# ScalarE divides the wide softmax tiles, and the engines' order is planned anew

## The chip, the core and the metric

The kernel runs on one core of a Trainium2 chip. A core has five engines that run their own queues of instructions in order and meet at semaphores: TensorE (PE in the profile; PEld is its weight load), VectorE (DVE), ScalarE (ACT), GpSimd (POOL) and SyncE (SP), which issues the DMAs. The metric is the time of one execution on the device, in microseconds.

## What is computed

One decoder layer on 512 rows of width 1024 in float32: a norm, one input projection into 17 parts, four groups of four attention heads of width 64, gates, and an output projection. Cut to what matters:

```python
hn = rms_norm(x, norm_gain)
proj = jnp.einsum('btd,de->bte', hn, w_in)
(fq, fk, fv, ff, fg, mq, mk, mv, mg, sq, sk, sv, sg, wq, wk, wv, wg) = split_columns(proj)
# f, m, w heads: s = q.k * scale + bias (forget sums, distance table, distance table in a window)
p = jax.nn.softmax(s, axis=-1).astype(v.dtype)
o = jnp.einsum('bhqk,bhkd->bhqd', p, v)
# s heads: a = exp(log_sigmoid(z) + suffix sums of log_sigmoid(-z)) below the diagonal
y = jnp.concatenate([from_heads(o_fox) * jax.nn.silu(fg), from_heads(o_moba) * jax.nn.silu(mg),
                     from_heads(o_sb) * jax.nn.silu(sg), from_heads(o_swa) * jax.nn.silu(wg)], axis=-1)
return x + jnp.einsum('bte,ed->btd', y, w_out)
```

In the softmax heads the division by the row sum is the step that the change is about.

## The kernel before

Each float32 operand of a large product is split into a high half (written by ScalarE in `hi_copy`, L137) and a low half (the difference, written by `lo_part` on VectorE, L142 or L144, or by GpSimd, L252). A product is then three matmuls (`mm3`, L340 to L342). The weights come in 39 chunks; for the chunks in `POOL_LO` GpSimd makes the low half in pieces of up to 260 columns, for all others VectorE does in one instruction. Names follow this: `wh_mqk0` and `wl_mqk0` are the halves of chunk 0 of the m heads' query and key weights, `raw_mqk0` what was loaded.

The work goes projection by projection (`ORDER`), and the heads of group s, then f, m and w run between the projections' matmuls. A head works through four query blocks. For block i of an f or m head the tile is 512, 384, 256 and 128 columns wide, for a w head at most 256. In `softmax_head` VectorE adds the bias and takes the row maximum (L548), ScalarE takes the exponential and its row sum (L550), VectorE takes the reciprocal of the sum (L555) and multiplies the tile by it (L556). The tile `pm` is then transposed on TensorE (`pT`, L522), split (`pth` by ScalarE, `ptl` by VectorE) and multiplied with V (`o`, L472 and L473). An s head has a chain of its own: scores on TensorE (`s_s`, L509 with the high half of k, L510 with the low half), three activations, a prefix sum by VectorE (`pm_s`, L592), a subtraction (L593) and an exponential (L594).

`pair_out` multiplies two heads' output by their gate on GpSimd (`oc`, L491) and splits it into `yh` (ScalarE) and `yl` (VectorE). The output projection starts with the six pairs of s, f and m (`out_tile`, tiles `o100`, `o101`, and so on) while the w heads run, and ends with the two pairs of w.

What the code writes down is not the order in which the engines run it. `order_engines` takes all instructions, and `_plan` lays them out anew, engine by engine, as a list schedule: each step has a cost from `_Step.cost`, a delay `_LAT` from engine to engine, an extra `MARGIN` for some receivers, and a priority, which is its place in the code plus an offset from `TURN`. A step may be taken before an earlier ready one if it can start within `PATIENCE` of it. VectorE and GpSimd read the on-chip memory through a port that they share; steps marked `port` take turns at it in the plan. The order found is then fixed by dependences, so that a table of numbers sets it.

Of the kernel before, what the change touches and what calls it, by code (L numbers as in the profile page):

```python
# [12 lines left out]
AF = mybir.ActivationFunctionType  # L13
ALU = mybir.AluOpType
# [24 lines left out]
REL_AT = "fg"  # L39
SQK_BANKS, R_BANK = ["sc", "tp", "tp", "pv"], "pj"  # L40

RATE, OUTU = 4.54, 0.55

POOL_LO = {1, 4, 6, 9, 10, 12, 15, 16, 17, 19, 21, 23, 24, 34, 36, 37, 38}
PIECE = 260
DVE_SQ = {(1, 1), (2, 1), (3, 0), (3, 1)}

OCUT, WARM, WARM_GAPS = 2, 3, 8


TURN = {"xn": 207, "gate": 18, "qk": -250, "v": -71, "s": 14, "pt": -313, "ot": 134, "gap":
        100000, "y": 10, "fb": 5, "w": 108, "pv": 16, "oc": 186, "nat": 0, "proj": 61, "x": -110}
PATIENCE = {"Pool": 10, "PE": 54}

MARGIN = {"PE": 100, "Activation": 41}


BOUNDS = list(range(17)) + [21, 27, 35, 46, 59, 77, 99, 128, 166, 216, 280, 363, 470]
# [18 lines left out]
def block_kernel(ctx, tc, x, xT, w_in, w_out, small, rel, out):  # L77
    nc = tc.nc
# [72 lines left out]
    if WARM:  # L151
# [3 lines left out]
        pt = pv("warm")  # L155
# [64 lines left out]
    def advance():  # L220
# [23 lines left out]
        for a0 in range(0, ka, ka // cut):  # L244
# [17 lines left out]
    xn = [[sb.tile([P, 512], F32, tag="yh", name=f"x{t}{h}", bufs=9) for h in range(2)]  # L262
          for t in range(NT)]
# [267 lines left out]
    def softmax_head(g, h, Q, K, V, vcol, bias, nblk):  # L531
        pm = sb.tile([P, 1280], F32, tag="pm", name=f"pm_{g}{h}", bufs=2)
        off, blocks = 0, {}
        for i in range(NT):
            w = nblk(i)
            n = w * P
            blocks[i] = (off, w)
            s, s2 = scores(g, h, i, n, Q, K)
            seg = pm[:, off:off + n]
            b = bias(i, n)  # L540
            if s2 is not None:
                nc.vector.tensor_tensor(seg, s2, b, op=ALU.add)
                b = seg
            nm = cp.tile([P, 1], F32, tag="nm", name=f"nm_{g}{h}{i}", bufs=4)
            sm = cp.tile([P, 1], F32, tag="sm", name=f"sm_{g}{h}{i}", bufs=4)

            init = nsk[:, h:h + 1] if g == "w" else 3.0e38
            nc.vector.tensor_tensor_reduce(seg, s, b, scale=-1.0, scalar=init,  # L548
                                           op0=ALU.add, op1=ALU.min, accum_out=nm)
            nc.scalar.activation(seg, seg, AF.Exp, scale=-1.0, bias=nm, accum_out=sm)  # L550
            if g == "w":
                es = cp.tile([P, 1], F32, tag="es", name=f"es_{g}{h}{i}", bufs=2)
                nc.scalar.activation(es, sk[:, h:h + 1], AF.Exp, bias=nm)
                nc.vector.tensor_tensor(sm, sm, es, op=ALU.add)
            nc.vector.reciprocal(sm, sm)  # L555
            nc.vector.tensor_scalar(seg, seg, sm, None, op0=ALU.mult)  # L556
            off += n
            yield
        for res in pt_tiles(g, h, pm, blocks):
            yield  # L560
        out_half(g, h, finish_head(g, h, res, V, vcol))
        yield
# [348 lines left out]
class _Step:  # L911
# [20 lines left out]
    def cost(self):  # L932
        n = self.writes[0].cols if self.writes else 1
        if self.eng == "PE":
            if "const" in self.reads[0].name:
                return n * 8 / 2.4
            if "float32r" in str(self.ins.ins[0].dtype):
                return n * 0.422 + 11
            return 112 if any("ident" in a.name for a in self.reads) else n * 4 / 2.4 + 11
        if self.kind == "DMACopy":  # L940
            return 1040 if self.eng == "Pool" else 60
# [94 lines left out]
def _plan(steps, moved, held_back, turn, patience, margin):  # L1036
# [23 lines left out]
    prio = [s.k + sum(turn.get(n, 0) for n in moved.get(s.ins.name, ())) for s in steps]  # L1060

    def start(e, k):
        t = max(free[e], ready[k])
        return max(t, port[other[e]]) if steps[k].port else t

    plan = []
    for _ in steps:
        t, e = min((start(e, k), e) for e in can for k in can[e])
        _, k, t = min((prio[k], k, start(e, k)) for k in can[e]
                      if start(e, k) <= t + patience.get(e, 0))  # L1070
        s = steps[k]
        can[s.eng].remove(k)
        src, end = s.eng, t + s.cost()
        plan.append((s, t, end))
# [68 lines left out]
```

## Time and profile before

| | us |
|---|---|
| median of 3 runs (lowest, highest) | 290.74 (290.61, 292.94) |
| the profiled execution | 290.52 |
| its span, first to last instruction | 288.7 |
| TensorE busy | 280.4 |
| VectorE busy | 233.6 |
| ScalarE busy | 193.8 |
| GpSimd busy | 89.5 |

The span is what the engines' instructions cover; the 1.8 us beside it lie before the first and after the last instruction. A matmul's row in the profile lasts longer than the time to the next one (0.39 us for 512 columns, where the next starts 0.23 us later), since matmuls are pipelined; short waits therefore do not show as idle time of PE, but as idle time of PEld, whose next load stands still.

### The profile page before, as it was taken

The page shows a single profiled execution, that of the slowest core. Times are in us where ns is not written, and L with a number is a line of the kernel's source. Part 1 is how long each engine was busy: PE and PEld are TensorE (multiplying, and loading weights), DVE is VectorE, ACT ScalarE, POOL GpSimd, SP SyncE. Part 2 cuts the span into 40 slices and gives each one's busy share as a digit, 9 for nine tenths or more (in the row PEclk, how much of TensorE's full clock was granted, in tenths as well). Part 3 has the DMA queues.
Part 4 walks back from the last instruction along what each step waited for, and adds up shares of the span by engine and source line. Part 5 has one row for each costly group of instructions (what it writes and reads, how often), then busy time and mean ns, then how long its engine had stood idle before and what let it go on. Part 6 is the DMA issues. An engine that isn't in the chain of part 4 may idle for free.

```text
span 288.7 us, 4641 instructions
## 1 busy us (share of the span) xinstructions
PE 280.4 (97%) x1529; PEld 235.9 (82%) x1529; DVE 233.6 (81%) x606; ACT 193.8 (67%) x445; POOL 89.5 (31%) x140
## 2 busy tenths in 40 slices
PE   8999998999999899999999999999999999999995
PEld 8998888888887678887798988788888886888884
DVE  2869289888998897669999789776989979996653
ACT  4784288957895947288895669569957877765300
POOL 5608045320029562135494000006200656001010
PEclk9999999999999999999999999999999999999999
DMA  7996342251023259621155240514001545200024
GB/s 236 333 400 191 116 151 76 70 176 44 0 74 105 95 152 287 171 73 38 41 143 148 73 145 2 183 36 145 3 18 72 173 138 168 89 2 0 2 110 182
DMA packets 19960, 33.65 MB, mean 117 GB/s; under 512 B 1616, under 2 KB 10068, under 8 KB 19808
## 3 DMA queue, kind: packets, MB, share of 16 engines
q1 hardware_dynamic: 19504, 32.96, 36.9%
q10 hardware_dynamic: 432, 0.39, 0.5%
q8 instruction: 12, 0.20, 0.3%
q14 instruction: 12, 0.10, 0.1%
HBM read 31.22 MB, written 4.22 MB: 123 GB/s over the span
## 4 chain that ended last, share of the span: by engine, by line
PE 68%; DVE 20%; ACT 8%; DMA 2%; issue 1%; ACTq 0%
PE o L342 5%; PE o L341 5%; PE o L340 4%; DVE pm_s L592 3%; PE p_wqkv L342 3%; PE p_wqkv L341 3%; PE p_wqkv L340 3%; PE p_sqk L341 2%; PE p_sqk L340 2%; PE p_sqk L342 2%; PE p_fqk L341 2%; PE p_fqk L340 2%; PE p_fqk L342 2%; DMA raw_sv<-in_w_in 2%; PE pT_m L522 2%; DVE pm_f L548 1%
## 5 line engine op out<-in xcount | busy, mean ns | idle before, releaser
L252 POOL TENSOR_TENSOR wl_fqk<-raw_fqk,wh_fqk 128x260 fp32r<-128x260 f32 (+1 forms) x12 | 11.8, 1010 | 18.9 <-ACT wh_fqk L137 18.9
L491 POOL TENSOR_TENSOR oc_f<-oc_f,gate_f 128x512 f32<-128x512 f32 x2 | 2.6, 1297 | 43.1 <-ACT gate_f L754 43.1
L676 POOL TENSOR_SCALAR fxb<-fbc,scol 128x512 f32<-128x512 f32 (+3 forms) x16 | 10.4, 654 | 17.4 <-DVE qs_f L144 10.4
L592 DVE TENSOR_TENSOR_SCAN pm_s<-l 128x512 f32<-128x512 f32 (+3 forms) x16 | 15.0, 942 | 0.1
L252 POOL TENSOR_TENSOR wl_sg<-raw_sg,wh_sg 128x256 fp32r<-128x256 f32 x8 | 7.0, 914 | 25.0 <-ACT wh_sg L137 25.0
L342 PE MATMUL p_fqk<-wh_fqk,xl 128*128 128x512 f32 x32 | 12.8, 401 | 0.0
L340 PE MATMUL p_mqk<-wh_mqk,xh 128*128 128x512 f32 x32 | 12.8, 400 | 0.0
L340 PE MATMUL p_wqkv<-wh_wqkv,xh 128*128 128x512 f32 x32 | 12.8, 399 | 0.0
L341 PE MATMUL p_mqk<-wl_mqk,xh 128*128 128x512 f32 x32 | 12.8, 399 | 0.0
L340 PE MATMUL p_fqk<-wh_fqk,xh 128*128 128x512 f32 x32 | 12.7, 403 | 0.0
L341 PE MATMUL p_fqk<-wl_fqk,xh 128*128 128x512 f32 x32 | 12.7, 397 | 0.0
L341 PE MATMUL p_wqkv<-wl_wqkv,xh 128*128 128x512 f32 x32 | 12.7, 396 | 0.0
L342 PE MATMUL p_mqk<-wh_mqk,xl 128*128 128x512 f32 x32 | 12.7, 396 | 0.0
L342 PE MATMUL p_wqkv<-wh_wqkv,xl 128*128 128x512 f32 x32 | 12.7, 396 | 0.0
L340 PE MATMUL p_sqk<-xh,wh_sqk 128*128 128x512 f32 x32 | 12.5, 389 | 0.0
L341 PE MATMUL p_sqk<-xl,wh_sqk 128*128 128x512 f32 x32 | 12.3, 390 | 0.0
L342 PE MATMUL p_sqk<-xh,wl_sqk 128*128 128x512 f32 x32 | 12.2, 392 | 0.0
L491 POOL TENSOR_TENSOR oc_w<-oc_w,gate_w 128x512 f32<-128x512 f32 x2 | 2.6, 1290 | 29.9 <-DVE oc_w L486 29.9
L142 DVE TENSOR_TENSOR ptl_s<-pT_s,pth_s 128x384 fp32r<-128x384 f32 (+3 forms) x16 | 7.4, 484 | 4.9 <-ACT pth_s L137 4.8
L142 DVE TENSOR_TENSOR ptl_m<-pT_m,pth_m 128x384 fp32r<-128x384 f32 (+3 forms) x16 | 7.3, 484 | 4.1 <-ACT pth_m L137 4.1
L137 ACT ACTIVATE pth_m<-pT_m 128x384 fp32r<-128x384 f32 (+3 forms) x16 | 6.5, 435 | 5.6 <-PE pT_m L522 5.4
L594 ACT ACTIVATE pm_s<-pm_s 128x512 f32<-128x512 f32 (+3 forms) x16 | 7.3, 465 | 4.1 <-DVE pm_s L593 3.9
(354 smaller groups left out, 1118.9 us busy)
## 6 DMA issues: line engine op xcount, KB each, us to landing
raw_o<-in_w_out SPq DMA_DIRECT2D x8, 512.0 KB, 3.2
xT<-in_xT SPq DMA_DIRECT2D x8, 256.0 KB, 4.1
raw_sqk<-in_w_in SPq DMA_DIRECT2D x4, 512.0 KB, 5.9
x<-in_x SPq DMA_DIRECT2D x8, 256.0 KB, 6.0
raw_fqk<-in_w_in SPq DMA_DIRECT2D x4, 512.0 KB, 3.7
raw_mqk<-in_w_in SPq DMA_DIRECT2D x4, 512.0 KB, 3.6
raw_wqkv<-in_w_in SPq DMA_DIRECT2D x4, 512.0 KB, 3.6
xr<-in_x SPq DMA_DIRECT2D x4, 512.0 KB, 3.8
```

What stands on the lines that cost most here:

```text
L137: nc.scalar.activation(dst, src, AF.Copy if isinstance(scale, float) else AF.Identity, scale=scale)
L142: nc.vector.tensor_tensor(dst, src, hi.bitcast(F32), op=ALU.subtract)
L252: nc.gpsimd.tensor_tensor(lv[q], rv[q], hv[q].bitcast(F32), op=ALU.subtract)
L340: nc.tensor.matmul(dst, ah, bh, start=first, stop=False)
L341: nc.tensor.matmul(dst, ah, bl, start=False, stop=False)
L342: nc.tensor.matmul(dst, al, bh, start=False, stop=last)
L491: nc.gpsimd.tensor_tensor(oc, oc, gates[e], op=ALU.mult)
L522: nc.tensor.transpose(pt[:, a * P:(a + 1) * P], pm[:, o:o + P], ident)
L548: nc.vector.tensor_tensor_reduce(seg, s, b, scale=-1.0, scalar=init, op0=ALU.add, op1=ALU.min, accum_out=nm)
L592: nc.vector.tensor_tensor_scan(seg, l, l, 0.0, ALU.add, ALU.bypass)
L594: nc.scalar.activation(seg, seg, AF.Exp)
L676: nc.gpsimd.tensor_scalar(b, bc[:, i * P:], -1.0, scol[:, i, h:h + 1], op0=ALU.mult, op1=ALU.add)
```

## The change

The diff does three things. In `softmax_head` tiles wider than 256 columns are multiplied by the reciprocal on ScalarE, with the reciprocal as the scale of an activation; these are the blocks of 512 and 384 columns of the eight f and m heads, 16 instructions. Of the chunks whose low half GpSimd makes, 6 (`fvf0`) and 17 (`mqk0`) go to VectorE and 32 (`o1`) comes from it (there is no chunk 39). And the planner gets other numbers: `TURN`, `PATIENCE`, `MARGIN` and `OUTU` change, a matmul of few columns costs more, and a step that takes the shared port waits `LEAD` longer before it on GpSimd. The instructions are otherwise the same; only their order changes. Lines of the changed file are numbered 2 higher before the new branch and 5 higher behind it.

```diff
--- before.py
+++ after.py
@@ -39,20 +39,22 @@
 REL_AT = "fg"
 SQK_BANKS, R_BANK = ["sc", "tp", "tp", "pv"], "pj"
 
-RATE, OUTU = 4.54, 0.55
-
-POOL_LO = {1, 4, 6, 9, 10, 12, 15, 16, 17, 19, 21, 23, 24, 34, 36, 37, 38}
+RATE, OUTU = 4.54, 0.4
+
+POOL_LO = {1, 4, 9, 10, 12, 15, 16, 19, 21, 23, 24, 32, 34, 36, 37, 38, 39}
 PIECE = 260
 DVE_SQ = {(1, 1), (2, 1), (3, 0), (3, 1)}
 
 OCUT, WARM, WARM_GAPS = 2, 3, 8
 
 
-TURN = {"xn": 207, "gate": 18, "qk": -250, "v": -71, "s": 14, "pt": -313, "ot": 134, "gap":
-        100000, "y": 10, "fb": 5, "w": 108, "pv": 16, "oc": 186, "nat": 0, "proj": 61, "x": -110}
-PATIENCE = {"Pool": 10, "PE": 54}
-
-MARGIN = {"PE": 100, "Activation": 41}
+TURN = {"xn": 207, "gate": 101, "qk": -250, "v": -54, "s": 14, "pt": -313, "ot": 322, "gap":
+        100000, "y": 7, "fb": 5, "w": 81, "pv": -31, "oc": 258, "nat": 0, "proj": 59, "x": -110}
+PATIENCE = {"Pool": 10, "PE": 54, "Activation": 29}
+
+MARGIN = {"PE": 100, "Activation": 52}
+
+LEAD = {"Pool": 120, "DVE": 0}
 
 
 BOUNDS = list(range(17)) + [21, 27, 35, 46, 59, 77, 99, 128, 166, 216, 280, 363, 470]
@@ -553,7 +555,10 @@
                 nc.scalar.activation(es, sk[:, h:h + 1], AF.Exp, bias=nm)
                 nc.vector.tensor_tensor(sm, sm, es, op=ALU.add)
             nc.vector.reciprocal(sm, sm)
-            nc.vector.tensor_scalar(seg, seg, sm, None, op0=ALU.mult)
+            if n > 256:
+                nc.scalar.activation(seg, seg, AF.Copy, scale=sm)
+            else:
+                nc.vector.tensor_scalar(seg, seg, sm, None, op0=ALU.mult)
             off += n
             yield
         for res in pt_tiles(g, h, pm, blocks):
@@ -935,7 +940,7 @@
             if "const" in self.reads[0].name:
                 return n * 8 / 2.4
             if "float32r" in str(self.ins.ins[0].dtype):
-                return n * 0.422 + 11
+                return max(n * 0.4167 + 15, 109)
             return 112 if any("ident" in a.name for a in self.reads) else n * 4 / 2.4 + 11
         if self.kind == "DMACopy":
             return 1040 if self.eng == "Pool" else 60
@@ -1060,15 +1065,20 @@
     prio = [s.k + sum(turn.get(n, 0) for n in moved.get(s.ins.name, ())) for s in steps]
 
     def start(e, k):
+
         t = max(free[e], ready[k])
-        return max(t, port[other[e]]) if steps[k].port else t
+        if not steps[k].port:
+            return t, t
+        t += LEAD[e]
+        return max(t, port[other[e]]), t
 
     plan = []
     for _ in steps:
-        t, e = min((start(e, k), e) for e in can for k in can[e])
-        _, k, t = min((prio[k], k, start(e, k)) for k in can[e]
-                      if start(e, k) <= t + patience.get(e, 0))
+        (t, _), e = min((start(e, k), e) for e in can for k in can[e])
+        _, k, t = min((prio[k], k, start(e, k)[0]) for k in can[e]
+                      if start(e, k)[0] <= t + patience.get(e, 0))
         s = steps[k]
+        t -= LEAD[e] if s.port else 0
         can[s.eng].remove(k)
         src, end = s.eng, t + s.cost()
         plan.append((s, t, end))
```

On VectorE, at the first scores of the s heads, before the change (qs_s and k are the low halves of queries and keys, sqk3 the last of the four projected tiles that they are made from):

```order
L144 SCALAR_TENSOR_TENSOR qs_s01_450<-sqk0_445,qs_s01_450 64x512
L144 SCALAR_TENSOR_TENSOR qs_s10_480<-sqk1_478,qs_s10_480 64x512
L144 SCALAR_TENSOR_TENSOR qs_s11_483<-sqk1_478,qs_s11_483 64x512
L142 TENSOR_TENSOR k00_138<-sqk2_511,k00_138 64x512
L142 TENSOR_TENSOR k01_140<-sqk2_511,k01_140 64x512
L786 TENSOR_TENSOR sqk3_574<-p_sqk3_519,rrow_135 128x512
L739 TENSOR_SCALAR fsp_151<-p_fvf0_582,rx_129 128x4
L586 TENSOR_TENSOR s_s00_612<-s_s00_612,smask_146 128x128
```

and after it:

```order
L146 SCALAR_TENSOR_TENSOR qs_s01_448<-sqk0_443,qs_s01_448 64x512
L791 TENSOR_TENSOR sqk3_572<-p_sqk3_517,rrow_135 128x512
L744 TENSOR_SCALAR fsp_151<-p_fvf0_580,rx_129 128x4
L146 SCALAR_TENSOR_TENSOR qs_s10_478<-sqk1_476,qs_s10_478 64x512
L146 SCALAR_TENSOR_TENSOR qs_s11_481<-sqk1_476,qs_s11_481 64x512
L144 TENSOR_TENSOR k00_138<-sqk2_509,k00_138 64x512
L144 TENSOR_TENSOR k01_140<-sqk2_509,k01_140 64x512
L144 TENSOR_TENSOR k10_142<-sqk3_572,k10_142 64x512
L144 TENSOR_TENSOR k11_144<-sqk3_572,k11_144 64x512
L146 SCALAR_TENSOR_TENSOR v_f0_606<-p_fvf0_580,rx_129,v_f0_606 128x4x64
L591 TENSOR_TENSOR s_s00_610<-s_s00_610,smask_146 128x128
```

The tile sqk3 and a small step of the forget gate now stand ahead of three more low halves, so k00 is made later in the row, and the mask of s_s00 stands behind k10, k11 and v_f0.

On TensorE, the second matmul of those scores (the one with k's low half) before:

```order
L341 MATMUL p_fvf1_636<-wl_fvf0_396,xh0_131 128x260
L342 MATMUL p_fvf1_636<-wh_fvf0_395,xl0_133 128x260
L340 MATMUL p_fvf1_636<-wh_fvf0_395,xh0_131 128x260
L510 MATMUL s_s00_612<-k00_138,qs_s00_447 128x512
L510 MATMUL s_s01_624<-k00_138,qs_s00_447 128x384
L341 MATMUL p_fvf1_636<-wl_fvf0_396,xh0_131 128x260
L342 MATMUL p_fvf1_636<-wh_fvf0_395,xl0_133 128x260
```

and after:

```order
L343 MATMUL p_fvf1_634<-wl_fvf1_527,xh1_132 128x260
L344 MATMUL p_fvf1_634<-wh_fvf1_526,xl1_134 128x260
L342 MATMUL p_fvf1_634<-wh_fvf2_538,xh1_132 128x260
L512 MATMUL s_s00_610<-k00_138,qs_s00_445 128x512
L512 MATMUL s_s01_622<-k00_138,qs_s00_445 128x384
L343 MATMUL p_fvf1_634<-wl_fvf2_539,xh1_132 128x260
L344 MATMUL p_fvf1_634<-wh_fvf2_538,xl1_134 128x260
```

That matmul and the next moved behind 15 further matmuls of the projection p_fvf1.

On VectorE, at the third s head (l_22 and l_23 are its last two blocks), before:

```order
L486 TENSOR_TENSOR oc_s0_808<-o_s1_972,lc_s1_981 64x512
L586 TENSOR_TENSOR s_s22_1049<-s_s22_1049,smask_146 128x128
L372 TENSOR_REDUCE qms_f3_1122<-sq_f3_1120 128x8
L582 TENSOR_TENSOR l_23_1136<-s_s23_1134,l_23_1136 128x128
L591 SCALAR_TENSOR_TENSOR l_22_1052<-s_s22_1049,l_22_1052 128x256
L748 TENSOR_TENSOR gate_f0_1227<-p_fg0_1202,rrow_135 128x512
L592 SCALAR_TENSOR_TENSOR pm_s2_1024<-l_22_1052 128x256
```

and after:

```order
L488 TENSOR_TENSOR oc_s0_806<-o_s1_970,lc_s1_979 64x512
L374 TENSOR_REDUCE qms_f3_1117<-sq_f3_1115 128x8
L285 TENSOR_SCALAR rmf3_1120<-qms_f3_1117,ex_130 128x8
L144 TENSOR_TENSOR wl_mqk0_1111<-raw_mqk0_1078,wh_mqk0_1110 128x1024
L596 SCALAR_TENSOR_TENSOR l_22_1050<-s_s22_1047,l_22_1050 128x256
L587 TENSOR_TENSOR l_23_1131<-s_s23_1129,l_23_1131 128x128
L753 TENSOR_TENSOR gate_f0_1222<-p_fg0_1197,rrow_135 128x512
L597 SCALAR_TENSOR_TENSOR pm_s2_1022<-l_22_1050 128x256
```

The low half of mqk0, one instruction of 1024 columns, now stands ahead of both blocks; before, GpSimd made it.

On TensorE, in the output projection while the first w heads run (wo5 holds a weight chunk, yh_m1 and yl_m1 the halves of the second m pair), before:

```order
L509 MATMUL s_w10_3197<-k00_138,qs_w01_2990 128x256
L510 MATMUL s_w10_3197<-k00_138,qs_w01_2990 128x256
L340 MATMUL o101_3119<-wo5_3059,yh_m1_3053 128x512
L341 MATMUL o101_3119<-wo5_3059,yh_m1_3053 128x512
L340 MATMUL o110_3161<-wh_o3_2844,yh_f1_2559 128x512
L342 MATMUL o100_3079<-wo5_3059,yl_m1_3054 128x512
L342 MATMUL o101_3119<-wo5_3059,yl_m1_3054 128x512
L341 MATMUL o110_3161<-wl_o3_2845,yh_f1_2559 128x512
```

and after:

```order
L342 MATMUL o100_3077<-wo5_3057,yh_m1_3051 128x512
L343 MATMUL o100_3077<-wo5_3057,yh_m1_3051 128x512
L344 MATMUL o100_3077<-wo5_3057,yl_m1_3052 128x512
L342 MATMUL o101_3110<-wo5_3057,yh_m1_3051 128x512
L511 MATMUL s_w10_3215<-k00_138,qs_w01_2988 128x256
L512 MATMUL s_w10_3215<-k00_138,qs_w01_2988 128x256
L343 MATMUL o101_3110<-wo5_3057,yh_m1_3051 128x512
L344 MATMUL o101_3110<-wo5_3057,yl_m1_3052 128x512
L344 MATMUL o110_3146<-wh_o2_2830,yl_f0_2550 128x512
```

The matmul with yl_m1 now stands right behind the two with yh_m1, ahead of o101's.

## Rows read from the trace of the kernel before

**Rows 1.** The page: busy time of each engine; granted clock in 40 slices
```profile
PE 280.4 (97%) x1529; PEld 235.9 (82%) x1529; DVE 233.6 (81%) x606; ACT 193.8 (67%) x445; POOL 89.5 (31%) x140
...
PEclk9999999999999999999999999999999999999999
```

**Rows 2.** Busy us of each engine in stretches of 10 us, then the sum
```profile
0.00:10.00 10.00, 8.77 (x51) 8.27 (x52) 4.60 (x11) 6.16 (x12) 4.25 (x17) 1.00 0.80 252
...
130.00:140.00 10.00, 9.80 (x46) 6.99 (x45) 9.81 (x33) 8.71 (x23) 5.88 (x14) 1.00 0.19 54
140.00:150.00 10.00, 10.00 (x65) 8.92 (x64) 10.00 (x40) 9.00 (x24) 6.89 (x14) 1.00 0.30 81
150.00:160.00 10.00, 9.76 (x74) 8.99 (x73) 9.94 (x29) 6.38 (x18) 4.48 (x7) 1.00 0.46 131
...
280.00:289.00 9.00, 5.45 (x30) 4.57 (x28) 3.60 (x6) 0.00 (x0) 0.00 (x0) 0.97 0.48 180
sum 289.00, PE 280.40 PEld 235.94 DVE 233.56 ACT 193.84 POOL 89.51; mean PE 9.67 PEld 8.14 DVE 8.05 ACT 6.68 POOL 3.09
```

**Rows 3.** Waits of TensorE's weight loads: us in total, times, longest
```profile
PEld pT_s L522 <- ACT pm_s L594: 1.8, 2, 1.0
PEld s_s L509 <- DVE pm_s L593: 1.2, 2, 0.9
PEld o L342 <- DVE yl_m L142: 1.1, 1, 1.1
PEld s_f L509 <- DVE nm_f L548: 1.0, 2, 0.5
...
PEld s_s L510 <- DVE k L142: 0.9, 1, 0.9
```

**Rows 4.** VectorE: the f heads' divisions (ns), and two of them in time
```profile
L556 DVE TENSOR_SCALAR pm_f<-pm_f,sm_f x16: 265/402/978, 134.9 to 163.3; 128x512 f32<-128x512 f32 x4, 128x384 f32<-128x384 f32 x4, 128x256 f32<-128x256 f32 x4, 128x128 f32<-128x128 f32 x4
...
140.62 0.46 DVE L556 TENSOR_SCALAR pm_f<-pm_f,sm_f 128x512 f32<-128x512 f32 x1
141.00 0.15 DVE L286 SCALAR_TENSOR_TENSOR rum<-r0m 128x8 f32<-128x8 f32 x1
141.08 0.40 DVE L556 TENSOR_SCALAR pm_f<-pm_f,sm_f 128x384 f32<-128x384 f32 x1
141.41 0.15 DVE L287 TENSOR_TENSOR rum<-rum,rmm 128x8 f32<-128x8 f32 x1
```

**Rows 5.** ScalarE in time: a scaled 512-wide copy, a 384-wide exponential, what follows each
```profile
8.86 0.72 ACT L137 ACTIVATE xh<-xT,small 128x512 fp32r<-128x512 f32 x1
9.49 0.40 ACT L137 ACTIVATE wh_sv<-raw_sv 128x256 fp32r<-128x256 f32 x1
...
134.02 0.60 ACT L550 ACTIVATE pm_f<-pm_f,nm_f 128x384 f32<-128x384 f32 x1
134.53 0.18 ACT L550 ACTIVATION_READ_ACCUMULATOR pm_f<-pm_f,nm_f 128x1 f32 x1
```

**Rows 6.** VectorE in time, scans and a weight split twice each; last row GpSimd
```profile
91.75 1.13 DVE L592 TENSOR_TENSOR_SCAN pm_s<-l 128x256 f32<-128x256 f32 x1
...
97.87 1.68 DVE L142 TENSOR_TENSOR wl_mqk<-raw_mqk,wh_mqk 128x1024 fp32r<-128x1024 f32 x1
...
109.23 0.69 DVE L592 TENSOR_TENSOR_SCAN pm_s<-l 128x256 f32<-128x256 f32 x1
...
111.07 1.23 DVE L142 TENSOR_TENSOR wl_mqk<-raw_mqk,wh_mqk 128x1024 fp32r<-128x1024 f32 x1
...
92.42 1.79 POOL L252 TENSOR_TENSOR wl_mqk<-raw_mqk,wh_mqk 128x252 fp32r<-128x252 f32 x2
```

**Rows 7.** VectorE in time around the first scores of the s heads
```profile
44.60 1.40 DVE L142 TENSOR_TENSOR k<-sqk,k 64x512 fp32r<-64x512 f32 x2
46.03 0.69 DVE L786 TENSOR_TENSOR sqk<-p_sqk,rrow 128x512 f32<-128x512 f32 x1
```

**Rows 8.** VectorE in time, the low half of the second m pair
```profile
240.05 1.31 DVE L142 TENSOR_TENSOR yl_m<-oc_m,yh_m 128x512 fp32r<-128x512 f32 x1
```

## The prediction

> **What bounds the kernel now.** I begin with the page. TensorE is busy for 280.4 us of a span of 288.7, and its granted clock reads 9 in all 40 slices [rows 1]. The clock is full from end to end, so it has nothing to give back; VectorE (233.6) and ScalarE (193.8) are far from full on the mean. The diff takes no matmul away and adds none. What it can change is the 288.7 − 280.4 = 8.3 us in which TensorE stands idle, and the waits too short to show as idle.
>
> The second view is busy time by stretches of 10 us. Of the 8.3 us, 10.00 − 8.77 = 1.23 lie in the first stretch and 9.00 − 5.45 = 3.55 in the last [rows 2], which are the first loads and the last output tiles; the order in front of me leaves these ends nearly as they are. Inside, some 3.5 us are left. A matmul's row is longer than its step (0.39 against 0.23 us), so each wait hides its first 0.16 us. With some twenty short waits that adds about 3 us; I estimate some 7 us of true waits inside. That is the most that any order can win.
>
> The third view, the waits of TensorE's weight loads, says where they are [rows 3]: two blocks of s heads' transposes wait 1.8 us for ScalarE, whose input comes from VectorE's scans; s heads' scores wait 1.2 and 0.9 for VectorE; one matmul of the output projection waits 1.1 for yl_m; two f heads' scores wait 1.0 for nm_f, VectorE's row maximum. Nearly every wait ends at VectorE or one step behind it. So VectorE is late in a few places rather than full, except in one: from 130 to 160 us, the f heads, it is busy 9.81, 10.00 and 9.94 of every 10, and ScalarE 8.71, 9.00 and 6.38 [rows 2].
>
> **The division.** Per head VectorE loses a multiplication of 512 and one of 384. In time, the first takes 141.00 − 140.62 = 0.38 us until the next instruction starts, the second 141.41 − 141.08 = 0.33 [rows 4]. Eight heads make 8 × 0.71 = 5.7 us off VectorE. ScalarE gets them. The trace of before has no such division on ScalarE; the nearest rows are a scaled copy of 512 columns, 9.49 − 8.86 = 0.63 us from start to start, and an exponential of 384 columns, 134.53 − 134.02 = 0.51 [rows 5]. I take these (both work on the same kind of tile from one-column operands), so 8 × 1.14 = 9.1 us come onto ScalarE. A head's chain grows by 0.25 and 0.18 us in its two wide blocks, plus the handover from VectorE's reciprocal to ScalarE, which was one engine before. The exponential and the transposes have other heads' work beside them, so I cost this chain at nothing where TensorE has such work, and at (0.25 + 0.18) × 4 = 1.7 us for the f heads if that cover is gone.
>
> In the f heads VectorE thus gets 4 × 0.71 = 2.8 us back of its 29.75 busy in 30. One of its 16 divisions there was stretched to 978 ns where the longest plain one takes about 0.46 [rows 4], so about 0.5 more comes back if that one no longer meets GpSimd at the shared port. What TensorE can win of it is bounded by what it shows lost: nm_f's 1.0 us, plus 0.20 + 0.00 + 0.24 of idle in the 30 us [rows 2, 3], 1.4 us in all. ScalarE's busy time goes from 24.1 to 24.1 + 4 × 1.14 = 28.7 of the 30 us, so part of the win goes into waits for ScalarE instead. I take −0.9, bounds −1.4 and +4.6 (the upper is the rival below). For the four m heads, which have no wait among the longer rows, I take −0.3 (bounds −1 and +1).
>
> **The low halves.** Weight chunks mqk0 (1,024 columns) and fvf0 come to VectorE, o1 leaves it. In the stretch from 91 to 98 us, before the third s head's end, GpSimd was making mqk's low half in pieces (1.79 us for two, so 3.6 us for four), and VectorE's rows beside it are stretched: a scan of 256 columns takes 1.13 us against 0.69 at 109, a weight split of 1,024 takes 1.68 against 1.23 at 111 [rows 6]. Four rows are stretched in this way there, 1.9 us in all; these are the first and the last of them, 0.44 and 0.45. After the change VectorE makes wl_mqk0 itself, 1.23 us by the unstretched row, ahead of both last blocks of that head, and gets the 1.9 back. That is 0.7 us earlier for the scan's followers, and the transposes that wait 1.8 us for them are also asked for somewhat later in TensorE's new order. I take −0.8, with bounds −1.8 (all of the wait goes) and +1.2 (the split is in the way and nothing is freed). The fvf0 split is costed at nothing: VectorE still waits for loads in the first 50 us, and TensorE asks for fvf0 later than it is made; uncovered it is 780/1,024 × 1.23 = 0.9. The o1 split goes onto GpSimd, 3.6 us by the same two pieces, in front of an output projection that it is needed for long after; GpSimd is busy 89.5 us in all, so at nothing too, and 1.23 comes off VectorE.
>
> **The order at the first scores.** Before, k00 is ready at 44.60 + 0.69 or so, and the matmul with k's low half waits 0.9 us for it. In the new order that matmul stands behind 15 more projection matmuls of 260 columns. At 0.23 × 260/512 = 0.117 us each it is asked for 1.75 us later. On VectorE sqk3 (0.69 us) and the small fsp now stand ahead of k00, which is thereby about 0.75 us later [rows 7]. 0.9 + 0.75 − 1.75 is below zero: the wait goes, −0.9, with bounds 0 and −1.5 (part of the wait of the first matmul, L509, would go with it). The mask of s_s00 comes behind k10, k11 and v_f0, some 2 us later than before, but TensorE itself is 1.75 us later there and the transposes of that head stand far behind: nothing; uncovered, +1.
>
> **The order at the output projection.** The row of yl_m lasts 1.31 us [rows 8], about twice the 0.70 of such a split of 512 columns (1.40 for two [rows 7]). TensorE's wait of 1.1 us is for it. Now the matmul with yl_m1 stands right behind those with yh_m1, that is 0.7 us earlier (three matmuls of 512), so TensorE asks sooner; on VectorE yl_m1 is moved ahead of a w head's row maximum and off the stretch, which by my count of the rows moves its end from 241.4 to about 239. I take −0.8, what shows of the wait beyond its hidden part; bounds −0.8 and 0.
>
> **The sum.** −0.9 (f) − 0.3 (m) − 0.8 (third s head) − 0.9 (first scores) − 0.8 (yl_m) = −3.7 us. All five sit inside a plan laid out anew over some 1,500 matmuls, and a different order has waits of its own at places where before had none. Before has about nine interior waits of over 0.3 us; the order after is as dense, and I add +1.5 us, three or four such waits (bounds 0 and +4). Net −2.2. Against the profiled execution, 290.52 us (its span and 1.8 us), this gives **288.3 us**; the median 290.74 lies 0.2 above, so about −0.8%. The bounds of the terms give 286.8 to 289.6 if they don't all fall on one side.
>
> **Rivals.** (1) *The waits only change places.* A list schedule that is nudged fills one gap and opens another; the port relief is small, since one f division in sixteen was stretched, and VectorE's load falls by only 5.7 + 1.23 − 1.23 − 0.9 = 4.8 us of 233.6. For it: TensorE is at 97% and every gain above is under 1 us. Against it: the gaps shown are longer than what the new order puts ahead of them. It gives 290.5 − 0.9 to 290.5 + 1.5, 289.6 to 292.0.
>
> (2) *All of it comes.* The five terms come whole and no new wait opens: 290.5 − 3.7 to −4.5, 286.0 to 286.8. For it: each term is read at its own wait. Against it: it needs an order without any new wait.
>
> (3) *ScalarE becomes the bound in the f heads: slower.* It decides if its queue comes to the copies of the transposed tiles (pth) later than TensorE asks for them. ScalarE would be busy 28.7 of 30 us. Each added division also stands in the queue until VectorE's reciprocal is there, and behind it wait the next exponential and the copy of another head's tile. If nothing of the added 4.6 us is covered, the stretch grows from 30 to 34.6, and with 2.5 of the other gains left or lost the time is 292.6 to 295.1. For it: 9.00 of 10 in the middle stretch already; against it: 6.38 in the last one, so room is there right behind.
>
> The Trainium skill speaks for this rival: "ScalarE: Activation LUTs", section "Rules for kernel authors", puts multiplications on VectorE and not on ScalarE, since VectorE is up to about three times as fast per element in bf16. These tiles are float32, and the rows here show 0.63 against 0.38 us, 1.7 times. At three times 0.38 and 0.33 the f heads would get 8.5 us instead of 4.6, 32.6 us of work in 30, and the time would be 293 to 295 by that rule; the rows say no, and I leave it 2 in 100 of the rival's chance.
>
> **How the numbers follow.** The forecast band of 286.8 to 289.6 gets 0.50, rival 1 0.27, rival 2 0.10, rival 3 0.13. The range from 286.0 to 292.0 holds the first three, 0.87, less what spills over each edge: about 8 in 10. One per cent, about what a measurement of this kernel can tell from no change, is 2.9 us: faster means below 287.8, slower above 293.65. Faster has rival 2's 0.10 and somewhat under half of the band, 0.23 in all; together 0.33. Slower has most of rival 3, 0.10. The rest, 0.57, is within.
>
> **What the profile after would show.** Right: no wait of 0.9 for k at L512 and none of 1.1 for yl_m at L344; VectorE at about 229 us, ScalarE at about 203, their rows of division 0.6 and 0.5 us apart from the next; the weight loads' wait for pm_s at the third s head under 1.0; TensorE's busy time unchanged and its idle inside under 2 us. Wrong: ScalarE at 9.8 or more of 10 through the f heads with weight loads waiting for pth_f or pm_f (rival 3), or the same total of waits under other names (rival 1). A row of division well over 0.7 us, a wait at the window or in the tail that my reading of the order missed, or VectorE's rows still stretched in the f heads would each break a term above.

## The result, and the profile after

The changed kernel takes 289.12 us (median of 15 runs) where the one before takes 290.67 (15 runs): a ratio of 0.9944, 95% interval 0.9929 to 0.9959, or 1.6 us less (1.2 to 2.1). The profiled execution took 289.2 us with a span of 287.4. The times of e3 and e9 below leave out executions that ran more than 1.5% above that kernel's fastest, three of e3's six (297.7 to 298.3 us) and one of e9's twelve (971.5 us).

The page of the changed kernel, busy time and granted clock:

```profile
PE 279.9 (97%) x1529; PEld 234.6 (82%) x1529; DVE 225.1 (78%) x591; ACT 202.1 (70%) x461; POOL 85.7 (30%) x137
...
PEclk9999999999999999999999999999999999999999
```

Against [rows 1] TensorE has the same matmuls and the same clock. VectorE gave up 8.5 us, more than the 4.8 of the prediction, and ScalarE took 8.3. The 16 divisions cost what the prediction said. ScalarE in time:

```profile
131.60 0.72 ACT L559 ACTIVATE pm_f<-pm_f,sm_f 128x512 f32<-128x512 f32 x1
132.23 0.60 ACT L552 ACTIVATE pm_f<-pm_f,nm_f 128x384 f32<-128x384 f32 x1
...
134.17 0.60 ACT L559 ACTIVATE pm_f<-pm_f,sm_f 128x384 f32<-128x384 f32 x1
134.68 0.39 ACT L552 ACTIVATE pm_f<-pm_f,nm_f 128x128 f32<-128x128 f32 x1
```

From start to start a wide one takes 0.63 us and one of 384 columns 0.51, as the nearest rows of before had it [rows 5]. The windows of the changed kernel (columns as in [rows 2]):

```profile
130.00:140.00 10.00, 9.94 (x50) 7.19 (x49) 8.72 (x36) 9.69 (x26) 5.50 (x14) 1.00 0.19 56
140.00:150.00 10.00, 9.73 (x63) 8.10 (x61) 9.94 (x35) 9.95 (x26) 7.02 (x13) 1.00 0.24 71
150.00:160.00 10.00, 9.90 (x76) 9.52 (x77) 8.67 (x24) 7.49 (x18) 2.76 (x4) 1.00 0.60 168
```

In the f heads VectorE is no longer full throughout, and ScalarE now is for 20 us: 9.69 and 9.95 of 10. TensorE's busy time there is 29.57 of 30 where it was 29.56: no gain shows. What TensorE's weight loads wait for, in the changed kernel:

```profile
PEld s_s L507 <- DVE pm_s L598: 1.3, 2, 1.1
PEld s_s L511 <- DVE pm_s L598: 1.2, 2, 0.7
...
PEld o_f L474 <- ACT pth_f L139: 0.7, 2, 0.5
PEld pT_f L524 <- DVE pm_f L561: 0.7, 2, 0.5
...
PEld pT_m L524 <- ACT pm_m L559: 0.7, 2, 0.4
PEld s_m L511 <- DVE nm_m L550: 0.7, 2, 0.4
PEld s_m L507 <- DVE nm_m L550: 0.7, 2, 0.4
PEld s_f L507 <- DVE nm_f L550: 0.7, 2, 0.4
...
PEld pT_f L524 <- ACT pm_f L559: 0.6, 2, 0.3
...
PEld pT_s L524 <- ACT pm_s L599: 0.5, 2, 0.3
...
PEld o L344 <- DVE yl_m L144: 0.4, 1, 0.4
```

Of the waits of before [rows 3], that of the scores for k's low half (0.9) is gone, that of pT_s for pm_s went from 1.8 to 0.5, and that for yl_m from 1.1 to 0.4. In their place stand new ones: 1.3 for pm_s at L507, in an s head, and the others mostly in f and m heads, for ScalarE's divided tiles (pm_m 0.7, pm_f 0.6), for its copies (pth_f 0.7) and for VectorE's maxima (nm_m 0.7 twice). The same view of before has one more row, which [rows 3] leaves out:

```profile
PEld pT_m L522 <- DVE pm_m L556: 1.0, 4, 0.4
```

TensorE thus waited 1.0 us for the m heads' divided tiles before the change too. After it, it waits 0.7 for ScalarE's and 0.3 for VectorE's: the engine changed, the total did not.

To see all waits, the hidden ones too, I added up over TensorE's matmuls what each start-to-start time has over the usual one of its size (0.2275 us for 512 columns, 0.174 for 384, 0.118 for 256, 0.109 for a transposition). The stages are cut at the same amount of matmul work in every kernel, near 20, 55, 112, 157 and 223 us. Worked out from the traces, in us (e1 to e12 are the runs of the next section):

```
                              start  first   s heads   f      m      w heads,
                                     scores  2 to 4    heads  heads  output    sum
before                        1.30   2.38    2.76      2.82   0.95   2.48     12.69
after                         1.08   1.11    2.08      3.20   1.97   1.48     10.92
e1  after's order, DVE div.   1.20   1.05    1.43      5.18   3.14   1.92     13.92
e2  before's order, ACT div.  1.26   2.93    2.89      5.15   2.77   3.32     18.31
e3  plan only                 0.81   1.11    1.44      4.61   2.26   5.90     16.13
e4  division only             1.69   2.38    2.79      2.44   1.71   5.12     16.12
e5  old f, m in new order     1.24   1.09    1.66      4.24   0.98   2.16     11.37
e6  new f, m in old order     0.78   2.36    2.96      3.70   3.58   1.94     15.31
e7  new first scores alone    1.18   1.09    3.18      3.50   0.93   2.52     12.40
e8  new s heads alone         1.55   2.47    2.05      4.97   1.02   2.52     14.58
e9  e8, sd ahead              1.03   2.37    1.63      3.09   0.95   2.52     11.59
e10 e5, sd ahead              1.56   1.10    2.20      3.74   0.89   2.25     11.75
e11 new output alone          1.61   3.70    2.68      2.81   0.95   2.23     13.99
e12 old m in new order        0.66   1.09    1.55      3.17   1.12   2.17      9.75
```

Each row is one execution. The first column moves by 0.9 us between kernels with the same order there (e2, e4, e6: 1.26, 1.69, 0.78), so it is not read. A column of a single kernel can be off by 0.6 or so, once by 1.3: e11 has the order of before at the first scores and shows 3.70 in that column, with a wait of 1.0 us for wh_sqk that before does not have in it. The last column of e3 and e4 also holds 1.6 and 1.7 us of lower clock, as told there. After against before: the first scores won 1.27, the third s head's stage 0.68, the output 1.00; the f heads lost 0.38 and the m heads 1.02. The sum, −1.77, is near the measured −1.6.

### The profile page after: what moved, and what is told of

It reads as the page before. It is cut to its first block, busy times and chain, and to the rows that moved or that the text cites. A ratio compares the mean times of both kernels' runs of the same rounds, so it can differ in the third digit from the quotient of the medians.

```text
span 287.4 us, 4634 instructions
## 1 busy us (share of the span) xinstructions
PE 279.9 (97%) x1529; PEld 234.6 (82%) x1529; DVE 225.1 (78%) x591; ACT 202.1 (70%) x461; POOL 85.7 (30%) x137
## 4 chain that ended last, share of the span: by engine, by line
PE 61%; DVE 19%; ACT 10%; DMA 5%; issue 2%; SPq 1%; DVEq 0%
PE o L343 4%; PE o L342 4%; PE o L344 4%; DVE pm_s L597 3%; DMA raw_sqk<-in_w_in 3%; PE p_wqkv L342 3%; PE p_wqkv L344 3%; PE p_wqkv L343 3%; PE p_sqk L342 2%; PE p_sqk L343 2%; PE p_sqk L344 2%; DVE l L596 2%; PE pT_m L524 2%; DMA xT<-in_xT 2%; PE p_mqk L344 1%
## 5 line engine op out<-in xcount | busy, mean ns | idle before, releaser
L254 POOL TENSOR_TENSOR wl_fqk<-raw_fqk,wh_fqk 128x260 fp32r<-128x260 f32 (+1 forms) x12 | 10.9, 935 | 23.0 <-ACT wh_fqk L139 23.0
L254 POOL TENSOR_TENSOR wl_sg<-raw_sg,wh_sg 128x256 fp32r<-128x256 f32 x8 | 8.2, 1059 | 24.0 <-DVE l L596 24.0
L681 POOL TENSOR_SCALAR fxb<-fbc,scol 128x512 f32<-128x512 f32 (+3 forms) x16 | 9.6, 606 | 10.7 <-DVE nm_f L550 6.2
L254 POOL TENSOR_TENSOR wl_o<-raw_o,wh_o 128x260 fp32r<-128x260 f32 (+1 forms) x8 | 6.6, 857 | 20.3 <-ACT wh_o L139 20.3
L254 POOL TENSOR_TENSOR wo<-raw_o,wo 128x260 fp32r<-128x260 f32 (+1 forms) x12 | 8.9, 780 | 4.3 <-ACT wo L139 4.3
L552 ACT ACTIVATE pm_m<-pm_m,nm_m 128x512 f32<-128x512 f32 (+3 forms) x16 | 8.9, 555 | 1.2 <-DVE nm_m L550 1.1
L552 ACT ACTIVATE pm_w<-pm_w,nm_w 128x256 f32<-128x256 f32 (+1 forms) x16 | 7.7, 479 | 2.9 <-DVE nm_w L550 2.5
```

The costliest lines, as they stand in the source:

```text
L254: nc.gpsimd.tensor_tensor(lv[q], rv[q], hv[q].bitcast(F32), op=ALU.subtract)
L681: nc.gpsimd.tensor_scalar(b, bc[:, i * P:], -1.0, scol[:, i, h:h + 1], op0=ALU.mult, op1=ALU.add)
```

## The experiments

**The division and the order, each without the other.** e1 keeps the changed kernel's order on all engines and moves only the 16 divisions into VectorE's row, where the plan had them in time; e2 does the reverse with the kernel before. The planner lays the division out for one engine, the instruction goes to the other (e1; in e2 the names are swapped):

```diff
-            if n > 256:
+            if n > 512:
                 nc.scalar.activation(seg, seg, AF.Copy, scale=sm)
...
+        self.real = self.eng
...
+        if self.div:
+            self.eng = "Activation"
...
-        if s.eng in last:
-            tc.add_manual_dep(s.ins, last[s.eng].ins.name, info, reason="order")
-        last[s.eng] = s
+        if s.real in last:
+            tc.add_manual_dep(s.ins, last[s.real].ins.name, info, reason="order")
+        last[s.real] = s
```

> The changed kernel's order on all five engines, word for word; only the 16 wide divisions are taken out of ScalarE's row and put into VectorE's row at the place in time that the plan gave them. Theory A (the prediction's: the division on ScalarE relieves VectorE in the f and m heads, 0.9 + 0.3 us of the gain): this kernel is 1.2 us slower than the changed one, 290.3 us, level with the kernel before within 0.4 us. Theory B (from the two traces: the gain comes at the first scores, the third s head and yl_m, while the weight loads of the f and m heads wait longer than before): it is no slower than the changed one, 287.7 to 289.2 us. Rival C (the order was laid out for ScalarE's division, so VectorE's runs badly in it): over 291 us.

Measured: 293.01 us, ratio to before 1.0067 (1.0041 to 1.0092); by the two ratios 3.6 us behind the changed kernel. Neither A nor B had this; C did.

> The order of the kernel before on all engines, word for word; only the 16 wide divisions go from VectorE's row to ScalarE's, at the place in time that the old plan gave them. Theory A: 0.5 to 1.2 us faster than before, 289.5 to 290.2 us. Theory B: no faster, 290.7 to 292 us, with waits for ScalarE (pm_f, pth_f) among the weight loads. Rival C: over 292 us, since ScalarE's row was not laid out for it.

Measured: 296.13 us, 1.0179 (1.0154 to 1.0205), 5.2 us slower. Again C. With the order that was laid out for it the division runs at 290.7 us on VectorE and 289.1 on ScalarE; in the other's order it costs 3.6 and 5.2 us. The weight loads of e2 show how, and below them two of ScalarE's rows in time:

```profile
PEld pT_m L522 <- ACT pm_m L557: 3.5, 3, 1.5
PEld o_f L472 <- ACT pth_f L137: 2.8, 4, 1.2
...
PEld pT_f L522 <- ACT pm_f L557: 1.5, 2, 0.9
```

```profile
142.65 1.22 ACT L557 ACTIVATE pm_f<-pm_f,sm_f 128x512 f32<-128x512 f32 x2
143.76 0.54 ACT L137 ACTIVATE pth_f<-pT_f 128x256 fp32r<-128x256 f32 x2
```

This is rival 3 of the prediction at its place: two divisions stand in ScalarE's queue ahead of the copies, and TensorE's matmul with pth_f starts at 144.19, 1.0 us late. ScalarE is not full for it: from 130 to 160 us it is busy for 26.8 us, where in the changed kernel it is for 27.1.

In e1 TensorE's longest wait in the f heads, 1.2 us, is for VectorE's ptl_f at 148.4. Two rows of VectorE just ahead of that step:

```profile
146.49 0.71 DVE L293 SCALAR_TENSOR_TENSOR r0m<-rum,r0m 128x8 f32<-128x8 f32 x1
147.13 0.89 DVE L561 TENSOR_SCALAR pm_f<-pm_f,sm_f 128x256 f32<-128x256 f32 x1
```

and the same two in the changed kernel:

```profile
146.62 0.16 DVE L293 SCALAR_TENSOR_TENSOR r0m<-rum,r0m 128x8 f32<-128x8 f32 x1
146.70 0.35 DVE L561 TENSOR_SCALAR pm_f<-pm_f,sm_f 128x256 f32<-128x256 f32 x1
```

Both are stretched in e1, by 0.55 us each. GpSimd at that time, in e1 and then in the changed kernel:

```profile
146.45 2.15 POOL L254 TENSOR_TENSOR wl_mg<-raw_mg,wh_mg 128x256 fp32r<-128x256 f32 x3
...
146.89 2.83 POOL L254 TENSOR_TENSOR wl_mg<-raw_mg,wh_mg 128x256 fp32r<-128x256 f32 x4 [0.27 <-ACT wh_mg L139]
```

and ScalarE, which writes the wh_mg that these pieces read, in the same order:

```profile
144.80 1.05 ACT L139 ACTIVATE wh_mg<-raw_mg 128x1024 fp32r<-128x1024 f32 x1
...
145.75 1.05 ACT L139 ACTIVATE wh_mg<-raw_mg 128x1024 fp32r<-128x1024 f32 x1
```

Without its divisions ScalarE comes to wh_mg 0.95 us earlier in e1. GpSimd's pieces therefore begin ahead of VectorE's two rows and not, as in the changed kernel, while the second of them is running. So an engine off the critical path that has less to do can set off work that meets another engine. This is read from the rows; no run tests it by itself.

**Either part, planned anew.** e3 is the changed kernel with every division on VectorE, e4 the kernel before with the wide ones on ScalarE; both let the planner lay everything out again.

```diff
-            if n > 256:
+            if n > 512:
```

> All of the changed planner's numbers and its list of GpSimd chunks, but every division on VectorE; the order is planned anew for that. Theory A: the three order terms remain, 0.9 + 0.8 + 0.8 less new waits: 289.8 to 290.3 us. Theory B: as fast as the changed kernel or faster, 288 to 289.3 us. A plan laid out anew can by itself open or close waits of some 1 us, so that e1 and not this run decides on the division.

Measured: 294.42 us (three executions), 1.0113 (1.0077 to 1.0148), 3.3 us slower than before. A had 290, B 289; both miss by far.

> The kernel before with nothing but the division of the wide tiles on ScalarE, planned anew with the old numbers. Theory A: 289.2 to 289.9 us. Theory B: 290.5 to 292 us. If it is level with the changed kernel (289.1), the planner's new numbers are worth nothing by themselves.

Measured: 293.47 us, 1.0082 (1.0049 to 1.0114), 2.4 us slower. By the table most of e4's loss is not in the heads that it changes (f 2.44 against 2.82, m 1.71 against 0.95) but in the last stage, the w heads, where no instruction changed: 5.12 against 2.48. Part of that is the plan, which fell out another way, and part is TensorE's clock. TensorE in e4 in time, then the stretch from 246 to 247 us (columns as in [rows 2]):

```profile
242.84 0.36 PE L509 MATMUL s_w<-k,qs_w 128*128 128x256 f32 x1 [1.09 <-DVE nm_w L548]
...
244.64 0.56 PE L340 MATMUL o<-wo,yh_m 128*128 128x512 f32 x1 [0.66 <-ACT yh_m L137]
245.00 0.63 PE L341 MATMUL o<-wo,yh_m 128*128 128x512 f32 x1
245.43 0.63 PE L340 MATMUL o<-wo,yh_m 128*128 128x512 f32 x1
```

```profile
246.00:247.00 1.00, 1.00 (x4) 0.81 (x3) 0.43 (x4) 0.00 (x0) 0.00 (x0) 0.50 0.00 0
```

Behind waits for nm_w and yh_m the granted clock is 0.50, which is 1.2 in place of 2.4 GHz, from 244.94 to 248.35 us. Matmuls of 512 columns then start 0.43 us apart and not 0.23, which adds 1.7 us. e3 has such a stretch too, from 234.54 to 237.95, behind a wait for pth_m, and it adds 1.6 us there. In no other trace here does the clock fall while TensorE still has work. e4 is slower even without it: the two executions with a mean clock of 1.0 took 292.07 and 292.49 us.

Of e3's loss, 2.5 us are one wait. In e3, VectorE in time, then GpSimd:

```profile
146.86 2.86 DVE L289 TENSOR_TENSOR rum<-rum,rmm 128x8 f32<-128x8 f32 x1
149.64 0.67 DVE L374 TENSOR_REDUCE qms_m<-sq_m 128x8 f32<-128x512 f32 x1
```

```profile
146.64 0.74 POOL L254 TENSOR_TENSOR wl_mg<-raw_mg,wh_mg 128x256 fp32r<-128x256 f32 x1
147.34 0.29 POOL L683 TENSOR_SCALAR_AFFINE_SELECT fxb<-fxb 128x128 f32<-128x128 f32 x1
147.60 2.10 POOL L254 TENSOR_TENSOR wl_mg<-raw_mg,wh_mg 128x256 fp32r<-128x256 f32 x3
```

An instruction of 8 columns, 0.15 us for the same one in [rows 4], lasts 2.86, until GpSimd's last piece ends; the division behind it is late, and with it TensorE's transposes. Another 2.3 us of e3 are the wait for pth_m ahead of the fallen clock. So a newly planned order cost 2.4 and 3.3 us, mostly at places that the edit did not touch and in part through the clock, and e3 and e4 do not price the parts.

**The changed order stage by stage.** For this I took the place of the planner by a table: the order of before and that of after are joined where both have issued the same matmuls (in the traces at TensorE's matmuls 330, 631 and 1260, behind the first scores, ahead of the f heads, behind the m heads). Such a join is called a seam below. Inside a stage each engine's row is then word for word that of one of the two.

```diff
-    for s, _, _ in _plan(_steps(tc.nc, slots), moved, held_back, TURN, PATIENCE,
-                         MARGIN):
+    steps = _steps(tc.nc, slots)
+    table = zlib.decompress(base64.b85decode(ROW))
+    for s in [steps[k] for k in struct.unpack("<%dH" % len(steps), table)]:
```

The low halves follow the stages (in e7 fvf0's, in e8 mqk0's goes to VectorE, in e11 o1's to GpSimd).

> The changed kernel's order on all engines up to the f heads and again from the w heads on; between them, in the f and m heads, the order of the kernel before, word for word, with every division on VectorE. Theory S (the stages' waits add up: in the f and m heads the changed kernel lost 1.4 us against before, elsewhere it won 3.2): 1.4 us faster than the changed kernel, 287.7 us, a ratio of 0.989 to before. Theory T (the stages hang together: heads that begin earlier find VectorE or the loads not ready and give it back): 289 us or more, no faster than the changed kernel.

Measured: 289.88 us, 0.9980 (0.9964 to 0.9997). T by its number; but the table has the m heads at 0.98 as in before and the loss in the f heads alone, for a reason that e8 shows.

> The mirror image: the order of the kernel before everywhere except in the f and m heads, which have the changed kernel's order with the wide divisions on ScalarE. It is the division with the order that was laid out for it, and nothing else. Theory S: 1.4 us slower than before, 292.2 us. The prediction's own terms (0.9 and 0.3 us won in the f and m heads): 289.6 us. Theory T: anywhere, with the loss at the seam behind the m heads.

Measured: 293.54 us, 1.0112 (1.0091 to 1.0134), T's case. Two waits of e6 stand at the seams, one ahead of the f heads and one at the end of the m heads:

```profile
PEld fTc L671 <- DVE fS L664: 1.4, 1, 1.4
...
PEld s_m L512 <- DVE nm_m L551: 1.7, 1, 1.7
```

The second is the row maximum of the last m head, behind wl_o, which the old list leaves on VectorE (1.22 us). With them e6 can't price the heads themselves: less 1.1 and 1.5 us of visible delay at these seams it has 2.6 in the f heads and 2.1 in the m heads, against 2.82 and 0.95 in before.

> The order of the kernel before except for the first 55 us, which have the changed kernel's order (with the low half of fvf0 on VectorE). The prediction's term for the first scores, 0.9 us: 289.9 us. Theory S, by the weight loads' waits in the two traces: 1.2 us won, 289.6 us. Theory T: the win is gone at the next scores, 290.9 us.

Measured: 290.24 us, 0.9993 (0.9976 to 1.0011). Its stage won all of 1.29 us, and the wait for k's low half is gone; the end came at most 0.7 earlier, where the prediction had 0.9 and S 1.2; T, with no gain, fits. In this trace the next two stages wait 0.42 and 0.68 more; the latter is a wait for ptl_f that e9 with the same order there does not have, so how much is really given back is open.

> The order of the kernel before except from 55 to 116 us, the second to fourth s heads, which have the changed kernel's order with wl_mqk0 on VectorE. The prediction's term for the third s head, 0.8 us: 290.0 us. Theory S, by the waits in the two traces: 0.6 us won, 290.2 us. Theory T: 290.9 us or more.

Measured: 292.15 us, 1.0067 (1.0038 to 1.0096). T by its number, but more was lost than had been won: the stage itself won 0.71 (2.05 against 2.76), and then the f heads lost 2.15. The cause stands on a queue that the prediction did not look at. SyncE's queue in e8 (what is issued, when, how many):

```profile
116.41 7.89 SPq L219 DMA_DIRECT2D raw_mg<-in_w_in  x2
124.74 0.27 SPq L664 DMA_DIRECT2D sd<-fS  x1
127.78 9.81 SPq L675 DMA_DIRECT2D fbc<-sd  x4
```

sd carries the f heads' forget sums out; their scan on VectorE had ended at 121.3. But sd stands behind the second load of raw_mg, and that load waits for a buffer that raw_mv held. ScalarE reads it for wh_mv, which the new order has at 119.92 (112.66 before), and GpSimd reads it last, for wl_mv:

```profile
121.06 2.84 POOL L255 TENSOR_TENSOR wl_mv<-raw_mv,wh_mv 128x256 fp32r<-128x256 f32 x4 [17.27 <-ACT wh_mv L140]
```

These pieces end at 123.90, and raw_mg is issued then. So sd is issued 3.4 us late, the broadcast fbc too, then GpSimd's fxb and VectorE's nm_f, and TensorE waits 1.7 us at the f scores. e9 and e10 move that one load behind sd and two fbc, as the changed kernel has it:

```diff
-DMA raw_mg<-in_w_in 128x4x256
 DMA sd<-fS 4x512
 DMA fbc<-sd 128x512
 DMA fbc<-sd 128x512
+DMA raw_mg<-in_w_in 128x4x256
```

> The kernel of e8 with one change: on SyncE's queue the transfers sd and the first two fbc (forget sums out and back, broadcast) stand ahead of the load of raw_mg's second chunk, as in the changed kernel; in e8 they stood behind it, and that load waited for ScalarE's wh_mv. Theory Q (e8's loss is that queue: sd was issued 3.4 us after its scan, so fxb and nm_f came late and f's scores waited 1.7 us): 290.0 us, 2 us faster than e8 and 0.7 faster than before, as the third head's weight loads already show. Theory T (the win of one stage is given back in the next whatever the queue): 291.5 us or more.

Measured: 289.94 us (eleven executions), 0.9983 (0.9962 to 1.0004), 2.4 us faster than e8 by the two ratios. Q, shown for e8's loss; that this kernel beats the one before is not, as the interval reaches no change. The queue in e9:

```profile
115.37 0.39 SPq L219 DMA_DIRECT2D raw_mg<-in_w_in  x1
120.29 0.28 SPq L664 DMA_DIRECT2D sd<-fS  x1
121.70 1.13 SPq L675 DMA_DIRECT2D fbc<-sd  x2
122.94 0.39 SPq L219 DMA_DIRECT2D raw_mg<-in_w_in  x1
```

> The kernel of e5 with the same move of sd and two fbc ahead of raw_mg's second chunk: the changed kernel's order up to the f heads and from the w heads on, the order of before in the f and m heads, all divisions on VectorE. Theory Q with S (stages add once the queue is mended): e5 waited 1.4 us more than before in the f heads; without that 288.3 us, 0.8 faster than the changed kernel, although ScalarE divides nothing. Theory T: 289.5 us or more. The prediction's terms for the f and m heads: 290.2 us.

Measured: 288.97 us, 0.9926 (0.9897 to 0.9955), against 289.12 and 0.9944 of the changed kernel: level with it (by the ratios 0.5 us faster, give or take 0.9). This is the kernel that decides on the division: ScalarE divides nothing in it, the f and m heads run in the old order, and the whole gain is there. A part of the gain under about 0.5 us could still be the division's.

> The order of the kernel before up to the end of the m heads, then the changed kernel's order for the w heads and the output projection (with o1's low half on GpSimd). The prediction's term for yl_m, 0.8 us: 289.9 us. Theory S, by the waits of this stage in the two traces (2.5 against 1.5 us): 289.7 us. Theory T: 290.7 us or more.

Measured: 290.51 us, 1.0002 (0.9975 to 1.0029): unclear, as the interval reaches from 0.7 won to 0.8 lost. In its trace the stage won 0.25, not 1.00. The wait for yl_m is 0.6 in it (0.4 in the changed kernel) and small waits follow the seam.

> The changed kernel with ScalarE's division and its order in the f heads, but in the m heads the order of the kernel before and every division on VectorE; the w heads and the output as in the changed kernel. Theory S (TensorE's waits in the m heads were 1.0 us before and 2.0 in the changed kernel; elsewhere nothing changes): 288.1 us, a ratio of 0.991, 1.0 us faster than the changed kernel. Theory T (the m heads find other engines late at the seam or hand the waits on to the output projection): 289.1 us or more. If ScalarE's division in the m heads was a gain, as the prediction had it with 0.3 us: 289.4 us.

Measured: 288.90 us, 0.9938 (0.9922 to 0.9954): level with the changed kernel. The m heads have 0.85 us less of waits (1.12 against 1.97), as S said, but the stage behind them 0.69 more (2.17 against 1.48, and 2.16 to 2.25 in the others with this seam). So T holds at the end: what the m heads won, the stage behind them did not use. Neither e10 nor e12 beats the changed kernel beyond the intervals.

## Why the prediction was right, and where it was not

**The time** was forecast at 288.3, a gain of 2.2; measured are 289.1 and 1.6. The gain came from where most of the sum put it, and the division, the change's own subject, had no part in it that e10 can tell. By the table the three order terms won 2.95 us where 2.5 were forecast. The f and m heads lost 1.40, where the division was to win 1.2 and 1.5 was set aside for new waits. That the time still fell into the band of 286.8 to 289.6 is in part luck: what the division did not bring was made up for in part by order terms that brought more.

- **First scores**, −0.9: the wait for k went, as worked out, and with parts of others the stage won 1.27 (1.29 in e7). By itself it moved the end by −0.2 (interval −0.7 to +0.3).
- **Third s head**, −0.8: 0.68 in the changed kernel, −0.5 (interval −1.1 to +0.1) at the end in e9. The reason given was half right. The low half of mqk0 on VectorE was to end the stretching at the port; but wl_mqk0 is itself stretched to 1.84 us, and another piece meets GpSimd later. VectorE in the changed kernel, then GpSimd:

```profile
88.40 1.84 DVE L144 TENSOR_TENSOR wl_mqk<-raw_mqk,wh_mqk 128x1024 fp32r<-128x1024 f32 x1
...
100.59 2.22 DVE L597 TENSOR_TENSOR_SCAN pm_s<-l 128x384 f32<-128x384 f32 x1
```

```profile
99.50 0.42 POOL L706 MEMSET relrow<- 4x384 f32 x1
99.88 2.10 POOL L254 TENSOR_TENSOR wl_mqk<-raw_mqk,wh_mqk 128x252 fp32r<-128x252 f32 x3
```

  A scan of 384 columns takes 0.95 us unstretched (54.05 in the same trace); here 2.22, and the new wait of 1.1 us for pm_s at L507 hangs on it. What won was, by the order, that the two transposes are asked for later (matmuls 506 and 530 of TensorE before, 512 and 536 after), less what this took; no run tests that alone. And the term left out SyncE's queue: with the old place of sd the new order of this stage makes the kernel 1.9 us slower (e8).
- **yl_m**, −0.8: the wait fell from 1.1 to 0.4, though its row is still stretched (1.17 against 1.31 [rows 8]); the stage won 1.00 in the changed kernel. That the row would come off the stretch is not what helped. Alone (e11) it shows no gain at the end.
- **The division**, −0.9 in the f and −0.3 in the m heads: this is the step that failed. VectorE was relieved by more than forecast, and TensorE's waits did not fall. In the f heads they are 3.20 against 2.82, inside the 2.81 to 3.74 that the old order there shows when sd is not late; in the m heads they grew by 1.02, clear of the 0.89 to 1.12 of the old order. The premise was that waits which end at VectorE go when VectorE has less to do. But e2 shows that the same relief in an order not made for it costs 5 us at ScalarE; and e10, with no relief at all, is as fast as the changed kernel. Nor was it right that the m heads had no wait among the longer rows: pT_m's 1.0 for pm_m was as long as nm_f's, and ScalarE's division kept it. The price on ScalarE (0.63 and 0.51 us) was right. The +1.5 of new waits was laid over the whole program; about that much (+1.4) lies in these two groups of heads.
- **Rival 3** did not come as a time in the changed kernel. Its sign came in part: ScalarE at 9.69 and 9.95 of 10 for 20 us, and waits of 0.7 for pth_f and 0.6 for pm_f. Its mechanism is shown in e2, at 296.1.
- **Rival 1** is refuted as a total, since it allowed a gain of 0.9 us at most and the interval begins at 1.2. As a description it fits the m heads, where waits changed their names and grew.
- **Rival 2**, all of it, needed 286.0 to 286.8 and is refuted.

That TensorE's idle time inside would fall under 2 us was wrong: of 287.4 − 279.9 = 7.5 us of idle the two ends (0.97 in the first 10 us, 3.7 behind 280) leave 2.8 (3.5 before).

What stays open: why single stages show less at the end (0.2, 0.5 and none; 0.7 in all) than the three together in e10 (2.2, interval 1.3 to 3.0). The intervals nearly allow it, and e8 shows one tie between stages. Inside a stage, the low half's move to another engine and the new order were not taken apart.

## What to carry to other kernels

When an engine waits for a busy neighbour, price the relief by the queues as they will be, not by busy time: here the same 16 divisions moved to the idler engine changed the time by −3.6 us in one order and +5.2 in another, and an order without the move was as fast. In a list-scheduled kernel whose TensorE is busy for 97% of the span, try a part inside a fixed order before believing a newly planned one, since two new plans cost 2.4 and 3.3 us, mostly at places that the edit did not touch. When a run is slower than its waits explain, look at the granted clock of each stretch: in e3 and e4 a fallen clock behind a wait cost 1.6 and 1.7 us more. When work moves on one queue, read which load on the DMA-issuing queue waits for a buffer that this work, or what follows it, frees, and what small transfer stands behind.

## What the runs showed of the hardware

VectorE's stretched rows are not bounded by one GpSimd instruction. The 8-column row of e3 lasted 2.86 us while GpSimd ran five instructions back to back (the longest some 0.74 us), and the 384-column scan of the changed kernel 2.22 instead of 0.95 beside three pieces of 2.10 us together; it ends 0.83 us after the last of them. The Trainium skill, "SBUF — State Buffer", section "SBUF: two separate sides", describes the pair of ports that the two engines share as a lock held for a whole instruction, with the other engine blocked fully. The rows agree that it is no sharing of bandwidth; that VectorE didn't get its turn between two GpSimd instructions goes beyond what the section says.
